# A hybrid encoder trunk on one core: the attention's first unit prepared among the last projections, the weights' tiles at the other end of memory, and the first block's squares added by VectorE

## The chip, the core and the metric

The kernel runs on one core of one Trainium2 chip. The metric is the device time of one execution in microseconds. Beside it stands one profiled execution, whose trace gives every instruction's start and duration on the engines: TensorE (PE), its weight loads (PEld), VectorE (DVE), ScalarE (ACT), GpSimd (POOL) and SyncE (SP), which issues the transfers here.

## The reference

One inference step of one layer over 2048 prompt tokens and 8 x 16 sample tokens, width 1024. One input projection of the normed tokens feeds three groups of heads: forgetting attention (FoX, 6 heads of 64, causal), an RWKV-7 recurrence (6 heads of 64) and cross-attention to 256 memory tokens (4 heads). Each is gated, and one output projection adds the result to the residual.

```python
h = rms_norm(x, norm_g) @ w_in
fox_cols, rwkv_cols, mem_cols = jnp.split(h, [FOX_COLS, FOX_COLS + RWKV_COLS], axis=-1)
# FoX: s = q k / 8 + cq - ck (c: cumulative log forget gates), causal mask, softmax, @ v
# RWKV: S <- S diag(w) + (S @ -kk) (kk a) + v k, y = S r, per-head norm, bonus
# memory: softmax(q mk / 8) @ mv
o = jnp.concatenate([o_f * jax.nn.silu(g_f), o_r * jax.nn.silu(g_r), o_m * jax.nn.silu(g_m)], axis=-1)
y = x + o @ w_out
```

The sample tokens do the same against cached keys and values (512 past rows, 256 memory rows) and a cached recurrent state. Keys, values, log forget gates and the final states are outputs too.

## The kernel before, in words

Precision is kept by splitting a float32 tensor into two parts, hi and lo (`fp32r`): hi is a cast on ScalarE, lo the difference on GpSimd or VectorE, and a product takes three matmuls. The kernel has two stages with a set of pools each.

**Stage 1, projections and recurrence** (pools `p1`, L123 to L942). A loop over four blocks of 512 tokens; the first has the 128 sample tokens as well, so 640. `prep_x` (L225 on) norms a block: squares, their sums over the width, a power, a broadcast back over the partitions, scaling (`stt`, L65) and the split (cast at L279, difference through `tt`, L62). For the first block the sums over partitions are made by PE: ScalarE squares each of the eight 128-row tiles (L251) and a matmul with a column of ones adds each into the tile `pq` (L253), first for 256 tokens, then for 384. `pb` is the broadcast back (L266) and `rb` its copy (L269). The other blocks square rows of tokens (L261). `wd_load` (L176 on) brings 256 columns of `w_in` in two halves of 1 MB, as hi and lo; the first block splits them (raw tile `wraw`, L200 to L202) and writes them to memory in `w_d`, from where the later blocks read them whole (L196). These tiles are in the pool `ws`, four of tag "hl". Projections are `pjd` (columns on the partitions, L209) and `pjt` (tokens on the partitions, `wide`). The columns of the RWKV heads go through `rwkv_in`, `rwkv_mid`, `rwkv_scan` and `rwkv_out` by pairs of heads; the other columns (FoX and memory queries, keys, values, gates) are spread among them. In the last block's last pair stand the memory's normed tokens (`memory_x`), its keys and values ("K", "V") and then the last two gate columns (`g` 0 and 128). `after`, `finish` and `output` close the stage: log forget gates, the last scan, its output.

The scan's PE instructions are named `pa` (first products), `sc` (the state's step), `sy` (its output), `yc` and `pss` (the head norm). The transfers `mk_d`, `mv_d`, `mq_d`, `q_d`, `k_d`, `v_d` and `fg_d` hold projected columns in memory between the stages.

**Stage 2, attention and output projection** (pools `p2`, L943 on). A unit is one pair of heads (`hp`) and 512 queries (`qb`); there are 12 FoX units and 8 of memory attention. A unit's preparation: `fox_keys` loads 512 keys as tokens (`tok`), PE turns them (`pt`, L1004), ScalarE and VectorE split them (L993, L994); `queries` does the same for the queries (L1071, L1072), then one matmul per 128 queries and 512 keys (`pm`) and a maximum over it (L1084 with the mask `mneg`, L1087 without), the maxima negated into `turnm` (L68), turned by PE (`pr`) and put into the queries' tile (L1115), where they are subtracted as part of the logits' matmul. Its main part, `attend`: logits `pS`, the mask, the exponential (L1143), its split (`Ph` by ScalarE, L1146; `Pl` by GpSimd, L62) and the products with the values (`po`). The output projection (`py`) is done for the first weights of w_out (`W`, L1331, tokens `oh`, L1349) early and for the others late; the samples' attention uses the past's keys and values (`sA`, `sB`).

**The order.** Units, memory units, samples and output projections are given fractions in a list `mix` that is sorted; after that `_arrange` puts every instruction of the whole program anew on its engine: a list schedule with a table of costs picks at each step the instruction that can start first, with the program's place as rank, several times over, and keeps the shortest. Tiles of a pool are handed over in the order in which they are asked for, and a pool of stage 2 that lies on the same memory as one of stage 1 waits for the instructions that use it.

## Time and profile before

| | |
| --- | --- |
| three runs | 1807.52, 1809.12 and 1819.66 us, median 1809.12 |
| profiled execution | 1797.65 us |
| its span, first to last instruction | 1795.9 us |
| mean granted clock of PE | 0.972 |
| PE, PEld busy | 94%, 76% of the span |
| DVE, ACT, POOL busy | 54%, 50%, 45% |
| stage 1 ends, stage 2 begins on PE | near 1134 and 1138 us |

A row of the timeline holds the start in the span, the busy time of the instructions taken together, the engine, the line, the operation, output from input, their shape and number (x), and in brackets how long the engine had been idle and what released it. A row of the groups ends with the busy time, the mean of one in nanoseconds, and the idle time before. Names of tiles are the program's. A matmul of `pq`, whose operands are full float32, is two passes in the trace; one of `pjd` is one.

### The profile page before, as it was taken

The numbers are of one execution on the slowest core, as the hardware profiler recorded it, in microseconds if no ns is written. First come the engines' busy times: TensorE is split into PE (matmuls) and PEld (weight loads), VectorE is DVE, ScalarE is ACT, GpSimd is POOL, SyncE is SP. The second block draws the span as 40 slices with busy tenths as digits, with TensorE's granted clock in tenths as the row PEclk, the third lists the DMA queues.
The fourth block names the chain that finished last, engine by engine and source line by source line (L and its number), as shares of the span: only waits on it lengthen the run. The fifth ranks groups of instructions, "written<-read, shape, count | busy, mean of one in ns | idle before, by whom it ended". The sixth has DMA issues, their size and how long they took to land.

```text
span 1795.9 us, 41000 instructions
## 1 busy us (share of the span) xinstructions
PE 1696.7 (94%) x16313; PEld 1362.8 (76%) x16313; DVE 978.1 (54%) x2295; ACT 897.9 (50%) x1783; POOL 811.8 (45%) x824
## 2 busy tenths in 40 slices
PE   7989999999999999999899999799999899999998
PEld 6989989687887788886688887466667666667776
DVE  4654655572454564354574372776745765675214
ACT  5424343523243524233324343588898778886552
POOL 3654543242322242131132151477788566866552
PEclk8999999999999999999999999799999999999999
DMA  6763846653644654644635654534445772444432
GB/s 196 267 202 117 269 144 206 209 178 120 212 156 142 244 184 159 198 155 140 204 109 168 195 160 132 166 121 154 128 149 169 251 251 89 138 142 157 154 111 106
DMA packets 236314, 303.11 MB, mean 169 GB/s; under 512 B 81594, under 2 KB 185976, under 8 KB 220250
## 3 DMA queue, kind: packets, MB, share of 16 engines
q1 hardware_dynamic: 236122, 300.49, 51.5%
q8 instruction: 128, 2.10, 0.5%
q14 instruction: 64, 0.52, 0.1%
HBM read 210.15 MB, written 90.28 MB: 167 GB/s over the span
## 4 chain that ended last, share of the span: by engine, by line
PE 37%; DMA 7%; DVE 7%; ACT 7%; issue 2%; POOL 2%; SPq 1%; DVEq 0%; POOLq 0%; ACTq 0%
PE py L59 8%; PE po L59 6%; PE pjd L59 6%; PE pS L59 5%; PE pjt L59 3%; PE pm L59 2%; ACT P L1143 1%; DMA inv_d<-yt 1%; ACT Ph L1146 1%; POOL Pl L62 1%; DMA sp_d<-spr 1%; DMA xd<-inv_d 1%; DMA rb<-rd 1%; PE pz L59 1%; PE sc L59 1%
## 5 line engine op out<-in xcount | busy, mean ns | idle before, releaser
L59 PE MATMUL pjd<-xk,w 128*128 128x512 f32 (+4 forms) x2280 | 540.2, 378 | 13.0 <-ACT xk L279 4.6
L59 PEld LDWEIGHTS pjd<-xk,w 128*128 128x128 f32 (+1 forms) x2280 | 386.5, 192 | 80.8 <-issue 10.5
L62 POOL TENSOR_TENSOR Pl<-P,Ph 128x512 fp32r<-128x512 f32 (+3 forms) x272 | 318.8, 1183 | 160.6 <-ACT Ph L1146 132.8
L59 PE MATMUL pjt<-w,xk 128*128 128x256 f32 x2040 | 291.4, 290 | 3.9 <-issue 3.9
L59 PEld LDWEIGHTS pjt<-w,xk 128*128 128x128 f32 x2040 | 265.6, 192 | 10.1 <-issue 4.1
L59 PE MATMUL py<-W,oh 128*128 128x512 f32 x816 | 242.6, 399 | 0.9 <-ACT W L1331 0.4
L1143 ACT ACTIVATE P<-pS,NB 128x512 f32<-128x512 f32 x240 | 147.5, 624 | 87.1 <-PE pS L59 34.4
L59 PEld LDWEIGHTS py<-W,oh 128*128 128x128 f32 x816 | 150.9, 189 | 40.1 <-issue 1.0
L59 PE MATMUL pS<-Q,K 128*128 128x512 f32 x480 | 156.6, 387 | 7.1 <-ACT P L1143 4.7
L1146 ACT CAST Ph<-P 128x512 fp32r<-128x512 f32 (+3 forms) x272 | 150.7, 564 | 11.0 <-PE po L59 6.2
L59 PE MATMUL po<-Ph,vt 128*65 128x512 f32 x480 | 153.5, 371 | 2.6 <-ACT ob L1166 1.7
L59 PEld LDWEIGHTS pS<-Q,K 128*128 128x128 f32 x480 | 86.0, 193 | 45.4 <-ACT P L1143 21.6
L1087 DVE TENSOR_REDUCE mx<-pm 128x1 f32<-128x512 f32 x144 | 95.7, 685 | 25.1 <-PE pm L59 23.7
L62 POOL TENSOR_TENSOR nr<-nr,mhalf 128x8 f32<-128x8 f32 (+2 forms) x43 | 62.3, 1448 | 100.3 <-DVE nr L68 87.7
L62 POOL TENSOR_TENSOR w<-wraw,w 128x1024 fp32r<-128x1024 f32 (+1 forms) x34 | 81.6, 2411 | 46.2 <-ACT w L201 33.4
L59 PE MATMUL pm<-K,Q 128*128 128x512 f32 (+2 forms) x240 | 91.2, 399 | 9.2 <-DVE mx L1087 4.0
L59 PE MATMUL po<-Pl,vt 128*65 128x512 f32 x240 | 88.3, 369 | 3.1 <-POOL Pl L62 2.9
L62 DVE TENSOR_TENSOR xo<-py,xo 128x512 f32<-128x512 f32 x68 | 46.2, 685 | 77.9 <-PE py L59 77.6
L59 PEld LDWEIGHTS po<-Ph,vt 128*65 128x65 f32 x480 | 63.4, 136 | 30.9 <-ACT ob L1166 3.3
L62 DVE TENSOR_TENSOR ytmp<-yt 64x14 f32<-64x14 f32 (+9 forms) x210 | 55.0, 262 | 41.8 <-DMA yt<-ld 37.1
L718 ACT COPY qk<-pjt 128x512 f32<-128x512 f32 (+1 forms) x47 | 26.1, 564 | 97.0 <-PE pjt L59 96.7
L59 PEld LDWEIGHTS pm<-K,Q 128*128 128x128 f32 x240 | 46.1, 195 | 31.8 <-DVE mx L1087 11.3
(401 smaller groups left out, 2843.8 us busy)
## 6 DMA issues: line engine op xcount, KB each, us to landing
w<-w_d SPq DMA_DIRECT2D x84, 1024.0 KB
w_d<-w SPq DMA_DIRECT2D x28, 1024.0 KB
y_d<-xo SPq DMA_DIRECT2D x21, 512.0 KB
wraw<-in_w_in SPq DMA_DIRECT2D x36, 256.0 KB
xo<-in_x SPq DMA_DIRECT2D x17, 512.0 KB
xo<-y_d SPq DMA_DIRECT2D x17, 512.0 KB
xt<-in_x SPq DMA_DIRECT2D x24, 256.0 KB
xraw<-in_xT SPq DMA_DIRECT2D x24, 256.0 KB
```

The source lines that it names most:

```text
L59: PE.matmul(out, lhsT, rhs, start=start, stop=stop, skip_group_check=True)
L62: e.tensor_tensor(out=out, in0=a, in1=b, op=op)
L718: S.copy(o_, out)
L1087: V.tensor_reduce(out=to, in_=pm[:, :n], op=MAX, axis=AX.X)
L1143: S.activation(P_[:, c0:], pS[:, c0:], AF.Exp, bias=NB[:, qb, 2 * hp + h, kt:kt + 1] if fox else 0.0)
L1146: S.copy(Ph[:, c0:], P_[:, c0:])
```

## The change

It has four parts.

1. **The first unit** (hp 0, qb 0) is prepared in stage 1. `fox_keys` is cut into `keys` and `values`; the helpers of `queries` take a table `where` that says which tiles they use, `first_` in stage 1 and `late_` in stage 2. `first_unit` gives stage 1's: the keys in one of the four "hl" tiles, the queries in the three `xraw` tiles and `rb`, the tokens in "qk", the mask in "w4", the maxima in "inv", the PSUM tiles in "pj". Keys and queries are emitted ahead of the last pair of gate columns; mask, maxima and negated rows after `after()`, ahead of the last `finish()`. The unit's values stay in stage 2.
2. **The pools** `ws` (weights) and `xr` (new: `xraw` and `rb`) are opened for the whole kernel at the right end of SBUF. Stage 2 uses their tiles: `sA` and `sB` in "hl", the raw output weights and residuals in "w", `ob`, `gt` and `rb2` in `xr`. The tiles of tag "big" fall from seven to five, `turnm` from four to three, the order of stage 2's pools changes.
3. **The first block's squares**: VectorE adds the eight squares of a half into one tile, and PE sums that tile alone, with two matmuls and then three in place of 16 and 24.
4. Smaller tiles: `ssq` halved, three buffers to two for `xss` of k, r and the small columns, two to one for `pb_`.

```diff
-PMB, PSB, PB, HB, LB, LAG, NKB, BIG, POB, PTB = 2, 2, 2, 5, 5, 3, 4, 7, 1, 3
+PMB, PSB, PB, HB, LB, LAG, NKB, BIG, POB, PTB = 2, 2, 2, 5, 5, 3, 4, 5, 1, 3
...
+    ws = pools(ctx, "ws", bufs=WHL, side="right")
+    xr = pools(ctx, "xr", side="right")
...
                     for k in range(KC):
                         sq = sqs[k // 5 if t0 else 0][:, k % 5 if t0 else k, :]
                         S.activation(sq, raws[k][:, c0:c1], AF.Square)
-                        for t in range(t1 - t0):
-                            mm(pq[:, t:t + 1], sq[:, 128 * t:128 * t + 128], one1, start=k + t == 0, stop=k == KC - 1)
+                        if k:
+                            tt(V, sqs[0][:, 0, :], sqs[0][:, 0, :], sq, A_)
+                    for t in range(t1 - t0):
+                        mm(pq[:, t:t + 1], sqs[0][:, 0, 128 * t:128 * t + 128], one1, start=t == 0)
...
+        def first_unit():
+            def k_tiles():
+                m = ws.tile([128, 2048], F32R, tag="hl", name="K0")
+                return [m[:, 512 * h:512 * h + 512] for h in range(2)], [m[:, 512 * h:512 * h + 512] for h in (2, 3)]
+
+            def q_tiles():
+                t_ = [xr.tile([128, 512], F32R, tag="xraw", name="Q0", bufs=3) for _ in range(3)]
+                t_.append(xr.tile([128, 512], F32R, tag="rb", name="Q0"))
+                return t_[:2], t_[2:]
...
+            load, *rest = queries(U0, q0, q_d[0:512, 0:128], 0, 0, True, first_)
+            return [lambda: first_keys[0](0, first_), load, masks, *rest]
...
                             wide(((w, 0), (w, 128)), memx, 2, 0)
+                        if j == len(mine) - 1:
+                            first = first_unit()
+                            for g in first[:2]:
+                                g()
                     f()
         after()
+        for g in first[2:]:
+            g()
         finish()
         output()
...
         def big(name, dtype=F32):
 
+            if name in ("sA", "sB"):
+                return ws.tile([128, 2048], dtype, tag="hl", name=name)
             return lt.tile([128, 2048], dtype, tag="big", name=name, bufs=BIG)
...
         for hp in range(3):
-            U = {}
-            block = fox_keys(U, hp)
+            U, q = ({}, {}) if hp else (U0, q0)
+            keys, values = fox_keys(U, hp) if hp else first_keys
             for qb in range(4):
-                pre, main, end = unit(U, hp, qb, True)
-                units.append(([lambda qb=qb, block=block: block(512 * qb)] + pre, main, end))
+                pre, main, end = unit(U, hp, qb, True, q if not hp and not qb else None)
+                step = [lambda qb=qb, keys=keys, values=values: (keys(512 * qb, late_), values(512 * qb))]
+                if not hp and not qb:
+                    step, pre = [lambda values=values: values(0)], []
+                units.append((step + pre, main, end))
```

The new order is the arranger's, so rows of it are shown, each with its line, operation, output from input and number; line numbers of the changed kernel differ from those of before.

PE at the program's start (`pq` the sums of squares, `pb` the broadcast, `pjd` the first projections). Before:

```order
L59 MATMUL pq<-one_82,xsq 128x1 x16
L59 MATMUL pb<-ident,rsq 128x128 x2
L59 MATMUL pq<-one_82,xsq 128x1 x15
L59 MATMUL pq<-one_82,xsq_247 128x1 x9
L59 MATMUL pjd<-xk,w 70x256 x7
L59 MATMUL pb<-ident,rsq 128x128 x3
L59 MATMUL pjd<-xk,w 70x256 x17
L59 MATMUL pjd<-xk,w 70x384
```

and now:

```order
L58 MATMUL pq<-one_82,xsq 128x1 x2
L58 MATMUL pb<-ident,rsq 128x128 x2
L58 MATMUL pjd<-xk,w 70x256 x4
L58 MATMUL pq<-one_82,xsq 128x1 x3
L58 MATMUL pjd<-xk,w 70x256 x5
L58 MATMUL pb<-ident,rsq 128x128 x3
L58 MATMUL pjd<-xk,w 70x256 x15
L58 MATMUL pjd<-xk,w 70x384
```

The first projections stand around the second half's sums and no longer behind 24 of them.

PE at the end of the last scan (`sc`, `sy`, `yc`, `pss` are the scan's, `pjd` the last pair's projections, 48 in all). Before:

```order
L59 MATMUL sy<-ya,ST 64x64 x2
L59 MATMUL sy<-ya,st 64x64 x14
L59 MATMUL sc<-st,AD 128x64
L59 MATMUL pjd<-xk,w 128x512 x2
L59 MATMUL yc<-yd,centre 128x512
L59 MATMUL pjd<-xk,w 128x512 x4
L59 MATMUL pss<-bones,yd 64x2 x8
L59 MATMUL pjd<-xk,w 128x512 x8
```

and now, with the first unit's transposes (`pt`):

```order
L148 MATMUL pt<-ident,tok 128x128
L58 MATMUL sc<-st,AD 128x64 x2
L58 MATMUL sy<-ya,ST 64x64 x2
L58 MATMUL sy<-ya,st 64x64 x14
L58 MATMUL sc<-st,AD 128x64
L58 MATMUL yc<-yd,centre 128x512
L58 MATMUL pss<-bones,yd 64x2 x8
L58 MATMUL pjd<-xk,w 128x512 x16
```

No projection stands between the scan's last steps now; all 48 follow `pss`. On SP, where the pair's two weight loads are issued (`w<-w_d`), before:

```order
L196 DMA w<-w_d 128x2048
L767 DMA fg_d<-gth 128x512
L196 DMA w<-w_d 128x2048
L726 DMA mk_d<-qk 128x2x256
L726 DMA out_mk_p<-qk 128x2x256
L767 DMA fg_d<-gth 128x512
L726 DMA mv_d<-qk 128x2x256
```

and now:

```order
L878 DMA mk_d<-qk 128x2x256
L878 DMA out_mk_p<-qk 128x2x256
L919 DMA fg_d<-gth 128x512
L145 DMA tok<-k_d 128x4x128
L878 DMA mv_d<-qk 128x2x256
L346 DMA w<-w_d 128x2048 x2
L145 DMA tok<-q_d 128x4x128
```

The loads stand behind the memory's keys and values and the first unit's key tokens.

ACT at the attention's beginning (`P` an exponential, `Ph` its cast, K and Q the casts of keys and queries, `W` of the output weights). Now:

```order
L1208 ACTIVATE P<-pS,NB 128x128
L1211 CAST Ph<-P 128x128
L137 CAST K_13952<-pt 64x512
L219 CAST Q_13989<-pt 64x512
L138 CAST K_13954<-pt 64x512
L220 CAST Q_13991<-pt 64x512
L1398 CAST W<-wr 128x1024
L137 CAST K_13953<-pt 64x512
```

where before, ahead of the first exponential:

```order
L993 CAST K_13963<-pt 64x512
L1013 CAST vt<-vtok 128x8x64
L994 CAST K_13965<-pt 64x512
L1071 CAST Q_14000<-pt 64x512
L1072 CAST Q_14002<-pt 64x512
L993 CAST K_13964<-pt 64x512
L1331 CAST W<-wr 128x1024
L1071 CAST Q_14001<-pt 64x512
```

The second unit's casts have moved from ahead of the first unit's exponentials to behind its eighth.

More of the change, by code (lines that the diff above doesn't have):

```diff
@@ new lines, in turned_in, with values_in @@
+    def turned_in(src, n, where):
+        t_ = where["tok"]()[:, :n // 128]
+        SY.dma_start(t_, src.rearrange("(t p) c -> p t c", p=128))
+        pt = where["pt"]("pt")
+        for t in range(n // 128):
+            PE.transpose(pt[:, 128 * t:128 * t + 128], t_[:, t, :], ident)
+        return pt
+    def values_in(vt, vsrc, nt):
+        t_ = c2.tile([128, 4, 2, 64], F32, tag="tok", name="vtok", bufs=3)[:, :nt]
+        SY.dma_start(t_, vsrc.rearrange("(t p) (h d) -> p t h d", p=128, d=64))
+        G.memset(vt[:, 0:130 * nt].bitcast(F32), 1.0)
+        v1 = vt[:, 0:130 * nt].rearrange("p (t h d) -> p t h d", h=2, d=65)
+        v2 = vt[:, 130 * nt:258 * nt].rearrange("p (t h d) -> p t h d", h=2, d=64)
+        S.copy(v1[:, :, :, 0:64], t_)
+        tt(V, v2, t_, v1[:, :, :, 0:64].bitcast(F32), SUB)
+        return v1, v2
@@ new lines, in fox_keys, with keys, values @@
+    def fox_keys(U, hp):
+        cs = slice(128 * hp, 128 * hp + 128)
+        U["K1"], U["K2"], U["vt"] = [], [], []
+        def keys(g0, where):
+            gs = slice(g0, g0 + 512)
+            pt = turned_in(k_d[gs, cs], 512, where)
+            k1, k2 = where["K"]()
+            for h in range(2):
+                split_keys(k1[h], k2[h], pt[64 * h:64 * h + 64], 512)
+                SY.dma_start(k1[h][64:67, :].bitcast(F32), nc_d[2 * hp + h:2 * hp + h + 13:6, gs])
+            U["K1"].append(k1)
+            U["K2"].append(k2)
+        def values(g0):
+            vt = kv.tile([128, 1032], F32R, tag="vt", name="vt", bufs=NKB)
+            U["vt"].append(values_in(vt, v_d[g0:g0 + 512, cs], 4))
+        return keys, values
@@ L168 @@
         xs_ = pools(p1, "xs")
-        ws = pools(p1, "ws", bufs=WHL)
         pj = pools(p1, "pj", bufs=3, space=bass.MemoryType.PSUM)
@@ L944 @@
         lt = pools(p2, "lt", bufs=2)
-        fill = lt.tile([128, FILL], BF16, tag="fill", name="fill", bufs=1) if FILL else None
+        kp = pools(p2, "kp")
+        wk = pools(p2, "wk", bufs=2)
+        lp = pools(p2, "lp", bufs=2)
         c2 = pools(p2, "c2")
@@ L1160, in values @@
                     if not R:
-                        R["ob"] = lt.tile([128, 512], F32, tag="ob", name="ob")
+                        R["ob"] = xr.tile([128, 512], F32, tag="xraw", name="ob", bufs=3)
                         R["sd"] = dt("sd", [2, 512], bufs=2)
@@ L1184, in ending @@
             def ending():
-                rb, gt = (lt.tile([128, 512], F32, tag=t_, name=t_, bufs=1) for t_ in ("rb2", "gt"))
+                rb, gt = (xr.tile([128, 512], F32, tag=t_, name=n_, bufs=b_) for t_, n_, b_ in (("rb", "rb2", 1), ("xraw", "gt", 3)))
                 SY.dma_start(gt, gsrc)
```

305 lines of the change are left out of this document (152 added, 153 removed).

## The prediction

> **What bounds the kernel now.** I read the shares of the page first, then the slices, then the table of windows over the two places that the change touches, then the timeline there.
>
> ```profile
> span 1795.9 us, 41000 instructions
> PE 1696.7 (94%) x16313; PEld 1362.8 (76%) x16313; DVE 978.1 (54%) x2295; ACT 897.9 (50%) x1783; POOL 811.8 (45%) x824
> PE   7989999999999999999899999799999899999998
> PEclk8999999999999999999999999799999999999999
> 20.00:30.00 10.00, 9.56 (x52) 9.30 (x52) 4.28 (x17) 2.05 (x5) 2.59 (x3) 1.00 0.69 207
> 30.00:40.00 10.00, 4.49 (x14) 2.84 (x14) 8.20 (x19) 8.15 (x22) 2.67 (x3) 0.71 0.54 180
> 40.00:50.00 10.00, 8.88 (x38) 7.53 (x39) 5.65 (x6) 5.53 (x12) 9.89 (x6) 0.61 0.80 256
> 50.00:60.00 10.00, 8.37 (x56) 8.14 (x56) 8.13 (x17) 5.41 (x13) 4.29 (x7) 1.00 0.99 341
> 1100.00:1125.00 25.00, 25.00 (x381) 21.31 (x380) 7.34 (x17) 7.93 (x17) 4.83 (x4) 1.00 0.46 149
> 1125.00:1150.00 25.00, 16.88 (x82) 12.16 (x81) 14.81 (x34) 13.35 (x27) 11.79 (x20) 0.73 0.68 210
> 1150.00:1175.00 25.00, 20.61 (x72) 13.01 (x73) 24.72 (x58) 17.70 (x37) 13.14 (x16) 0.72 0.34 110
> 1175.00:1200.00 25.00, 24.37 (x121) 16.95 (x120) 16.30 (x37) 22.65 (x41) 17.53 (x17) 1.00 0.38 116
> ```
>
> PE is busy 94% of the span, so only places where it idles or runs below its full clock can give time. The slices show few: the first, and the one with a 7 in both rows near two thirds. A window's row holds its length, the busy time of PE, PEld, DVE, ACT and POOL, the granted clock, and the share and rate of the DMA. PE's busy time times its clock over 1125 to 1175 is 16.88 x 0.73 + 20.61 x 0.72 = 27.2 us of 50, so some 23 us are lost where the projections hand over to the attention. From 30 to 50 it is 4.49 x 0.71 + 8.88 x 0.61 = 8.6 of 20. From 50 on, and again from 1175 on, PE is nearly full at full clock. The change works on both holes.
>
> **Part 1: the first block's squares.** Now every square is summed over the 128 partitions by PE; 40 such matmuls are 80 passes in the trace.
>
> ```profile
> 4.57 6.98 PE L59 MATMUL pq<-one,xsq 128*128 128x1 f32 x32 [4.57 <-ACT xsq L251]
> 10.10 0.52 ACT L251 ACTIVATE xsq<-xraw 128x384 f32<-128x384 f32 x1 [0.52 <-DMA xraw<-in_xT]
> 14.25 1.28 DVE L65 SCALAR_TENSOR_TENSOR xraw<-xraw,vec,rb 128x256 f32<-128x256 f32 x3 [2.51 <-ACT rb L269]
> 14.27 10.40 PE L59 MATMUL pq<-one,xsq 128*128 128x1 f32 x48 [0.46 <-ACT rb L269]
> 24.54 1.75 PE L59 MATMUL pjd<-xk,w 128*70 128x256 f32 x7
> 33.74 0.40 PE L59 MATMUL pjd<-xk,w 128*70 128x384 f32 x1 [4.18 <-ACT xk L279]
> 39.62 5.01 POOL L62 TENSOR_TENSOR w<-wraw,w 128x1024 fp32r<-128x1024 f32 x2 [3.21 <-ACT w L201]
> 51.11 6.18 PE L59 MATMUL pjd<-xk,w 128*128 128x384 f32 x39 [0.90 <-DVE fl L62]
> ```
>
> The two pq rows are 17.38 us for 80 passes, 0.217 each; 10 passes remain, 2.2 us, so PE gives up 15.2 us. VectorE takes 14 adds; its nearest row is 1.28 / 3 = 0.43 us for 128x256, and by width 0.64 at most for 128x384, so 7 x 0.43 + 7 x 0.64 = 7.5 us, on an engine that is busy for 4.28 us of 10 from 20 to 30. They run behind the squares one by one, so that of each half only the last add, 0.4 and 0.6, lies on the path.
>
> What it brings is not 15.2, since other things must be there. In the first half the sum is ready when PE has drained, at 4.57 + 6.98 = 11.55. ScalarE has by then done squares of the second half (10.10). In the changed order the last token tile of the first half is loaded behind two loads of the second and squared behind one square of the second, so I put its square at about 9.4 and its add at 9.9: a gain of 1.7 us. The second half: the pq passes end at 24.67, and the first 128x384 projection begins at 33.74; without the passes it can begin near 26, so 7.7 us sooner. Next in line is the split of the next weights on Pool (39.62 to 44.63), which itself waits for ScalarE's cast of them and those for the tokens' tiles; if it moves with the rest, to about 37.5, it gains 7.1. From 51.11 PE is full, so whatever is gained there is kept. The term is **-7.1 us**. Bounds: 0 if a transfer sets the pace (the DMA share is 0.99 at 341 GB/s from 50 to 60), and the whole 10.40 us of the second pq row on the other side.
>
> **Part 2: the hand-over.** The first unit's keys, queries and eight maxima are made among the last pair's projections, in their tiles. The cover it takes away is that of the last scan. I count from the last scan's first "pa" matmul ("pa" at 1110.78, with as much PE work left on both sides).
>
> ```profile
> 1082.80 0.79 PE L59 MATMUL pjd<-xk,w 128*128 128x512 f32 x1 [3.08 <-DMA w<-w_d]
> 1076.74 0.54 SPq L196 DMA_DIRECT2D w<-w_d  x1
> 1110.78 1.15 PE L59 MATMUL pa<-bt,za 64*64 64x64 f32 x32
> 1118.86 0.36 SPq L726 DMA_DIRECT2D mv_d<-qk  x1
> 1125.00 0.63 PE L59 MATMUL pss<-bones,yd 128*64 128x2 f32 x16
> 1129.95 4.13 PE L59 MATMUL pjd<-xk,w 128*128 128x512 f32 x17
> 1138.08 1.11 PE L1004 MATMUL pt<-ident,tok 128*128 128x128 f32 x4 [4.00 <-DVE gth L65]
> 1146.60 0.30 DVE L1084 CUSTOM_DVE_ANT_0 pm<-pm,mneg 128x128 f32<-128x128 f32 x1
> 1152.59 0.13 DVE L1084 DVE_READ_ACCUMULATOR2_ANT mx<- 128x1 f32 x1
> 1157.97 0.69 ACT L1143 ACTIVATE P<-pS,NB 128x512 f32<-128x512 f32 x1 [2.10 <-DVE pS L62]
> 1172.80 2.53 PE L59 MATMUL py<-W,oh 128*128 128x512 f32 x7
> 1178.02 0.48 PE L59 MATMUL pS<-Qm,Km 128*128 128x512 f32 x1
> ```
>
> A pass of the last pair costs 4.13 / 17 = 0.243 us. Before, 16 of its 48 passes fill the scan's waits and the last ends at 1134.08, 23.3 after pa. In the changed order none of the 48 stands ahead of pss, because the pair's two weight loads are issued behind mv_d (1118.86); a load of that kind was used 1082.80 - 1076.74 = 6.1 us after its issue, so the first half is there 14.2 after pa. pss ends at 1125.63, 14.9 after pa, and then come 48 x 0.243 = 11.7 and four transposes of 0.28: the last pass ends 27.7 after pa, **4.4 later** than before.
>
> What follows it is shorter. Before, 23.9 us pass from the last pass to the first exponential (1157.97): tokens back from memory, transposes, casts, maxima. Now the casts are done by then; left are the first maximum's matmul (1.1), eight maxima (VectorE's own work between 1146.60 and 1152.72, without the pauses for PE and for a scan of the sample's forget values, is 3.5), and from the last maximum to the first exponential as before, 1157.97 - 1152.72 = 5.3: 9.9 together, so 14.0 saved. The first exponential comes 27.7 + 9.9 = 37.6 after pa and not 47.2: **9.6 sooner**.
>
> That isn't the gain, for the second unit's preparation moves the other way. Before, its keys' and queries' eight casts and two of w_out's stand on ScalarE ahead of the first exponential. Now they stand behind the first unit's eighth. By the rows
>
> ```profile
> L1143 ACT ACTIVATE P<-pS,NB 128x512 f32<-128x512 f32 x240 | 147.5, 624 | 87.1 <-PE pS L59 34.4
> L1146 ACT CAST Ph<-P 128x512 fp32r<-128x512 f32 (+3 forms) x272 | 150.7, 564 | 11.0 <-PE po L59 6.2
> 1139.23 0.58 ACT L993 CAST K<-pt 64x512 fp32r<-64x512 f32 x1 [0.49 <-PE pt L1004]
> 1148.55 1.04 ACT L1331 CAST W<-wr 128x1024 fp32r<-128x1024 f32 x1
> ```
>
> eight exponentials with their casts are at most 8 x (0.624 + 0.564) = 9.5 (narrower ones less: I take 9), and the ten casts 8 x 0.58 + 2 x 1.04 = 6.7. So the second unit's casts, its maxima and its exponentials wait for 9 of the 9.6 and come 0.6 sooner than before. The early output projections (py, 1172.80) need only the last two of these casts and could begin some 5 sooner; the first memory logits (1178.02) stand behind the second unit's casts on ScalarE and follow them. What counts is when PE is full for good, which the memory logits mark: I take **0 us**. Bounds: -9.6, if PE finds work beside the second unit's casts, and +9: the 4.4 lost, and half of the 9 besides.
>
> **Part 3: the attention.** Pools at memory's other end let the past's keys and values (sA, sB) start loading in the last projections, where before
>
> ```profile
> 1400.00:1425.00 25.00, 21.23 (x106) 13.90 (x105) 22.93 (x61) 17.80 (x37) 13.23 (x18) 0.86 0.91 286
> PE pS L59 <- DMA sB<-in_cmkT: 0.7, 2, 0.5
> ```
>
> the window with their use loses 25 - 21.23 = 3.8 us of PE at DMA share 0.91, of which the wait itself shows 0.7. Against it stand five big tiles where there were seven, so that a memory unit's queries can't be prepared two ahead. PE's order in the rest is the same by units. I take **-1**: from -3.8, the window's whole loss, to +3.8, as much again where a memory unit's queries come late. Edits without a time of their own: masks read as two planes, smaller rows for squares, one buffer less for shifted columns; they are small beside the scans that hide them, and would cost a VectorE instruction's 0.3 each if not.
>
> **Sum.** -7.1 + 0 - 1 = -8.1. On the profiled execution's 1797.65 (span 1795.9 and 1.75 around it) that is 1789.6. The median of the runs is 1809.12, 11.5 above the profiled one, with 12 us between the lowest and the highest; so I subtract from the median: **1801.0 us**.
>
> [...] The row after the 4.00 us wait above is
>
> ```profile
> 1140.00:1145.00 5.00, 2.73 (x10) 1.75 (x8) 3.24 (x5) 4.06 (x9) 2.91 (x7) 0.50 1.03 294
> 1155.00:1160.00 5.00, 4.93 (x16) 3.42 (x15) 4.92 (x12) 2.46 (x5) 0.86 (x1) 0.50 0.38 111
> ```
>
> half clock from 1140 to 1160, 20 us. [...]
>
> **Rivals.** A, the hand-over pays in full (PE has the first unit's values, py and transposes to do while ScalarE casts): -7.1 - 9.6 - 1 = -17.7, 1791.4. For it: py's rows could begin 5 us sooner. Against: VectorE was 24.72 of 25 busy from 1150 to 1175, so it is no free engine there.
> B, the start gives only its first 1.7: the weights' loads and ScalarE's squares of the second block set the pace there; -1.7 + 0 - 0 = 1807.4. For it: ScalarE 8.15 of 10 and the DMA at 0.99. Against: the 4.18 us wait was for xk, not for a transfer.
> C, slower: the last pair's weights. Their loads queue behind mv_d with the first unit's own tokens and w_out's; if the first lands 6 us later than I say, PE has no work after the scan, and the 48 passes run at half clock, 11.7 us more: 6 + 11.7 - 7.1 - 1 = +9.6, 1818.7. It decides once PE idles over 4 us ahead of the pair. Against: the DMA share there is 0.46 from 1100 to 1125.
> D, the planner puts the maxima behind everything anyway, and only part 1 works: -7, which is the forecast's time.
>
> **How the numbers follow.** Forecast (with D) 0.50, A 0.25, B 0.14, C 0.11. A spread of 5 us around each is the runs' own. The range 1784 to 1818 takes in A, B and the bounds of part 1, and leaves out the far side of A and most of C. A measurement here tells about 1% from no change, 18 us. Over 1% faster is half of A, and the forecast with both of its terms at their good bounds: 0.29. Over 1% slower is the tail of C: 0.12. Within 1%: 0.59.
>
> **What would show it.** In the profile after: pq passes 10, the first 128x384 projection near 26 and PE full from about 44; the last pair's passes in one run behind pss, its clock 1.00; the first exponential about 10 us nearer to the last scan, and the first memory logits no nearer. It is wrong if the last pair waits for its weights (C), if the memory logits come 8 us sooner too (A), or if the wait for xk near 30 stands with another name (B).

## The result, and the profile after

| | before | after |
| --- | --- | --- |
| median of four runs each, on one chip | 1808.85 us (1807.52 to 1819.66) | 1827.32 us (1824.57 to 1830.33) |
| profiled execution, its span | 1797.65, 1795.9 us | 1824.57, 1822.8 us |

The ratio is 1.0088, interval 1.0062 to 1.0114: 16 us slower by the ratio, and 18.5 by the medians. I had said 8.1 faster, with 1784 to 1818 as the range. The loss is under 1%, but its interval lies wholly above 1, the sign is not the one I gave, and the time lies outside the range.

The page of the kernel after: the busy shares, and PE's two rows of slices.

```profile
PE 1691.6 (93%) x16243; PEld 1347.3 (74%) x16243; DVE 984.0 (54%) x2309; ACT 895.1 (49%) x1784; POOL 805.1 (44%) x824
PE   5789997989999999999989999879999999999998
PEclk9899998999999899999999999889999999999999
```

PE has 5 us less to do (1691.6 against 1696.7) and the span is 26.9 longer, so what grew is the time in which PE idles; the mean granted clock is 0.972 in both. Three places show in the slices: the first two (5 and 7, where there were 7 and 9), the seventh (7 at clock 8, at 273 to 319 us) and the hand-over (8 and 7).

The start, in two of the windows that the prediction used for before: length, busy time of PE, PEld, DVE, ACT and POOL, granted clock, DMA share and rate.

```profile
40.00:50.00 10.00, 6.90 (x32) 5.90 (x32) 4.19 (x7) 0.81 (x3) 3.81 (x2) 0.72 0.58 190
50.00:60.00 10.00, 3.28 (x12) 3.19 (x13) 6.86 (x18) 6.69 (x15) 5.49 (x6) 0.62 1.05 382
```

PE was to be full from about 44; from 50 to 60 it is busy for 3.28 of 10 at clock 0.62, where before it had 8.37 at 1.00. The rows of the timeline of after, PE and ACT, in the order of time:

```profile
30.29 0.59 PE L58 MATMUL pjd<-xk,w 128*70 128x384 f32 x1 [1.85 <-ACT xk L431]
49.91 1.04 ACT L351 CAST w<-wraw 128x1024 fp32r<-128x1024 f32 x1 [3.23 <-DMA wraw<-in_w_in]
50.98 0.47 ACT L468 COPY fsb<-pjd 6x384 f32<-6x384 f32 x1
51.51 0.34 PE L471 MATMUL pf<-ident,fsb 6*128 6x6 f32 x3 [4.17 <-ACT fsb L468]
57.07 3.25 PE L58 MATMUL pjd<-xk,w 128*128 128x384 f32 x9 [5.22 <-DVE xsk L64]
```

The first wide projection does begin 3.4 sooner (30.29 for 33.74). Then PE waits 4.17 us for `fsb`, a small copy on ScalarE that stands in its queue behind a cast of weights; that cast had itself waited 3.23 for its transfer. Behind it PE waits 5.22 more, and is full from 57.07 and not from 51.11.

The next place lies between 200 and 400 us, on which the prediction said nothing. The two windows of before, and those of after:

```profile
200.00:300.00 100.00, 97.79 (x1199) 91.77 (x1199) 60.50 (x143) 40.12 (x85) 46.61 (x43) 1.00 0.59 194
300.00:400.00 100.00, 94.97 (x1139) 77.98 (x1137) 56.54 (x145) 39.62 (x89) 28.73 (x32) 0.97 0.59 188
```

```profile
200.00:300.00 100.00, 90.37 (x1112) 82.38 (x1108) 46.32 (x122) 37.30 (x80) 40.92 (x39) 0.93 0.56 178
300.00:400.00 100.00, 87.27 (x1009) 72.20 (x1010) 51.05 (x131) 36.01 (x84) 18.39 (x24) 0.93 0.48 159
```

Busy time by clock is 189.9 before and 165.2 after. What is late there is seen in the view of one tile, `xssk` (a pair's shifted sample columns; each row has its least, median and longest time, and the start of the first and the last of the three pairs). `bk` is the last to read it. Before, then after:

```profile
L307 POOL COPY xssk<-shp x3: 200/202/672, 56.5 to 213.5; 128x8 f32<-128x8 f32 x3
L65 DVE SCALAR_TENSOR_TENSOR bk<-xssk,vh,e x3: 350/350/1090, 322.1 to 842.8; 128x128 f32<-128x128 f32 x3
```

```profile
L459 POOL COPY xssk<-shp x3: 199/201/207, 64.8 to 332.5; 128x8 f32<-128x8 f32 x3
L64 DVE SCALAR_TENSOR_TENSOR bk<-xssk,vh,e x3: 350/352/353, 332.1 to 869.5; 128x128 f32<-128x128 f32 x3
  DVE bk L64: 5.5, 1
```

All three pairs write such a tile in the first block, and the first pair's is read when its sample unit runs, behind the third pair. With three buffers the third write stands at 213.5, with two at 332.5, right behind the first pair's `bk` at 332.1: the last row says that Pool sat idle 5.5 us for that `bk`. So the third pair's samples, written 119 us later, hold back the end of the first block. The next block's tokens, the eight casts of `xk` of 512, tell by how much. Before, then after:

```profile
L279 ACT CAST xk<-xraw x8: 609/619/621, 311.9 to 337.8; 128x512 fp32r<-128x512 f32 x8
```

```profile
L431 ACT CAST xk<-xraw x8: 602/618/622, 360.4 to 379.6; 128x512 fp32r<-128x512 f32 x8
```

The first is 48 us later. This is the smallest edit of the change, the one that the prediction put among those "without a time of their own".

To set whole kernels beside each other I cut each trace where PE has done the same amount of matmul work (sums of squares left out, each shape at the duration that it has back to back). The reference is a second run of the kernel before, `b_same` below, since its profiled execution of 1797.65 lies 11 under the median; its cuts are at 63.8, 219.8, 427.3, 1124.5 and 1206.9 us of 1802.0. With other durations for the shapes an entry moves by up to some 3 us. Microseconds lost (+) or gained (-) against it:

| kernel | to 64 | to 220 | first block's end, to 427 | to 1124 | hand-over, to 1207 | attention | span |
| --- | --- | --- | --- | --- | --- | --- | --- |
| before, first profile | +2.1 | +0.3 | +0.2 | -10.2 | +0.2 | +1.2 | -6.1 |
| after | +9.8 | -0.3 | +14.9 | -4.6 | +8.1 | -7.1 | +20.8 |
| after_t14 | -0.5 | -0.9 | +12.3 | +6.0 | +12.0 | +0.1 | +29.0 |
| after_t4 | +1.9 | -2.7 | +15.0 | -3.7 | +11.3 | +2.3 | +24.0 |
| a_xss3 | +5.7 | -7.5 | -3.1 | -20.8 | +11.2 | +5.9 | -8.6 |
| a_xss3_t5 | +2.2 | +1.3 | -1.4 | -16.4 | +9.2 | -3.7 | -8.8 |
| a_xss3_unit1 | +2.7 | +3.1 | -0.8 | -16.6 | +9.7 | +4.7 | +2.8 |
| a_xss3_late | +1.9 | +3.6 | -2.3 | -14.5 | +2.5 | -2.7 | -11.7 |
| a_xss3_pq | +1.9 | +2.9 | -1.6 | -8.3 | +12.3 | +6.0 | +13.1 |
| a_xss3_kept | +8.9 | -0.3 | +13.2 | -2.1 | +12.2 | -5.1 | +26.8 |
| a_samp01 | +2.9 | +4.5 | -5.0 | +4.5 | +8.0 | +4.5 | +19.3 |
| a_samp01_t16 | +1.2 | +1.8 | -3.4 | -13.5 | +7.3 | +0.7 | -5.9 |
| a_pq | +2.1 | +6.9 | +18.4 | +1.9 | +8.2 | +3.5 | +41.1 |
| b_xss2 | +3.6 | 0.0 | +9.3 | -6.3 | -2.9 | +2.2 | +5.9 |
| b_adds_xss2 | +1.3 | +1.8 | +7.9 | -1.3 | -1.1 | +12.8 | +21.5 |
| b_adds | +6.8 | -2.3 | -6.7 | -9.6 | -1.5 | -2.7 | -16.0 |
| b_adds_t4 | +1.0 | +2.8 | -2.2 | -5.6 | -0.1 | +1.3 | -2.8 |
| b_adds_kept | -0.7 | +3.4 | -2.2 | -2.1 | -0.1 | +3.6 | +1.9 |
| b_try2 | +0.9 | +9.8 | -3.8 | -13.2 | +3.9 | +5.3 | +3.1 |

The first row is the same program twice: 10 us in one column is within what a run does.

### The profile page after: what moved, and what is told of

Its sections match the earlier page's. It is cut to its first block, busy times and chain, and to the rows that moved or that the text cites. A ratio compares the mean times of both kernels' runs of the same rounds, so it can differ in the third digit from the quotient of the medians.

```text
span 1822.8 us, 40919 instructions
## 1 busy us (share of the span) xinstructions
PE 1691.6 (93%) x16243; PEld 1347.3 (74%) x16243; DVE 984.0 (54%) x2309; ACT 895.1 (49%) x1784; POOL 805.1 (44%) x824
## 4 chain that ended last, share of the span: by engine, by line
PE 56%; DMA 12%; DVE 10%; ACT 8%; issue 4%; SPq 2%; POOL 2%; DVEq 0%; ACTq 0%; POOLq 0%
PE pjd L58 15%; PE py L58 8%; PE pjt L58 7%; PE po L58 7%; PE pS L58 4%; PE pm L58 2%; ACT P L1208 2%; DMA w<-w_d 2%; PE sc L58 1%; ACT Ph L1211 1%; DMA AR<-sp_d 1%; PE gr L58 1%; PE pz L58 1%; DMA yd<-sp_d 1%; DMA inv_d<-yt 1%
## 5 line engine op out<-in xcount | busy, mean ns | idle before, releaser
L58 PE MATMUL pjd<-xk,w 128*128 128x512 f32 (+5 forms) x2280 | 551.0, 382 | 40.0 <-DMA w<-w_d 7.1
L58 PEld LDWEIGHTS pjd<-xk,w 128*128 128x128 f32 (+1 forms) x2280 | 390.4, 193 | 112.1 <-issue 12.8
L58 PE MATMUL pS<-Q,K 128*128 128x512 f32 (+1 forms) x480 | 156.4, 389 | 8.6 <-ACT P L1208 5.6
L235 DVE TENSOR_REDUCE mx<-pm 128x1 f32<-128x512 f32 x144 | 95.5, 684 | 27.7 <-PE pm L58 26.7
L61 POOL TENSOR_TENSOR xk<-xraw,xk 128x512 fp32r<-128x512 f32 (+2 forms) x20 | 23.8, 1188 | 82.4 <-ACT xk L431 82.4
```

Of the source, the lines that this page charges most:

```text
L58: PE.matmul(out, lhsT, rhs, start=start, stop=stop, skip_group_check=True)
L61: e.tensor_tensor(out=out, in0=a, in1=b, op=op)
L235: V.tensor_reduce(out=to, in_=pm[:, :n], op=MAX, axis=AX.X)
```

## The experiments

**Theories.** One: two buffers for `xss` of k, r and the small columns make the first block end late, and that is the loss. Two: the first unit's early preparation costs it in the hand-over, because the second unit comes late. Three: neither, but the order that `_arrange` happens to keep, since any edit changes it everywhere. The expectations call one A, three B and two H; their C is that the adds and what they do to the start are the cost. Names with b_ are the kernel before with an edit, those with a_ the changed kernel. Medians are those of the runs, each ratio is against before on the same chip, and a comparison of two kernels rests on their medians.

### Buffers and adds, each alone and undone

`b_xss2` takes the two buffers into before, `b_adds` the adds, `b_adds_xss2` both. `a_xss3` gives the changed kernel its third buffer back (for room, the first unit's negated rows lie in a scan tile, and stage 2 has three of its own), `a_pq` takes the adds out, `a_xss3_pq` does both.

```diff
-name="xss" + key, bufs=3)
+name="xss" + key, bufs=3 if key in "gv" else 2)
...
+            rows0 = rw.tile([128, 512], F32R, tag="e5", name="rows0")
```

> The kernel before with one edit: the tiles of the sample tokens' shifted columns (xss of k, r and the small columns) have two buffers and not three. Theory A (the two buffers are what cost stage 1 its time: the third pair's sample columns must wait until the first pair's sample unit has read its own, and the order of the whole first block bends around that): slower than before by 15 to 20 us, about 1826, with the loss between 200 and 400 us of the span. Theory B (any edit makes the arranger pick another order and the changed kernel's loss is chance): anywhere from 10 us faster to 20 slower, with the loss in no fixed place. Theory C (the adds on VectorE and what they do to the start are the cost): no change within 4 us.

> The kernel before with the first block's squares added by VectorE and summed by 5 matmuls, nothing else changed. Theory A: the adds are not the loss; from no change to 7 us faster (the first projections at 30 us sooner, a part of it kept). Theory B: anywhere within 20 us. Theory C: 8 us slower or more, with ScalarE's copy of the forget columns behind a cast that waits for its weights, near 50 us.

> The changed kernel with three buffers again for xss of k, r and the small columns; to make room, the first unit's negated rows and the rounded identity lie in a scan tile (e5) and stage 2 has its own again. Theory A: 15 to 20 us faster than the changed kernel, 1807 to 1812, with stage 1 as long as before and the hand-over still some 10 us longer. Theory B: anywhere within 20 us of the changed kernel. Theory C: as the changed kernel, 1827, within 4 us.

> The changed kernel with the 40 sums on PE as before and no adds on VectorE. Theory A: within 5 us of the changed kernel, 1822 to 1832, since the loss of the first block stays. Theory B: anywhere within 20 us. Theory C: 8 to 15 us faster than the changed kernel, 1812 to 1819, with PE full from 51 us as before.

> The changed kernel with three buffers for xss of k, r and the small columns (1795.9 us so far) and the first block's sums on PE as before, no adds. If the adds are worth some 17 us in every surrounding (they were 16.5 on the kernel before and 17.6 on the changed one): 1811 to 1815. If that was chance of the order, with the adds' own effect read at the start alone (3 to 8 us lost there): 1786 to 1794.

> The kernel before with the adds (1790.8 us so far) and two buffers for xss of k, r and the small columns. Theory A (the third pair's sample columns wait for the first pair's sample unit, whatever stands around): 14 to 31 us slower than with three, 1805 to 1822, the loss between 200 and 300 us of the span. If the two buffers cost 5 us, as the median on the kernel before had it: 1796.

| other parts of the change | sums by | three buffers | two buffers |
| --- | --- | --- | --- |
| none | PE | 1807.4 (before) | 1813.3, 1.0023 [0.9996, 1.0051] |
| none | VectorE | 1790.8, 0.9894 [0.9856, 0.9933] | 1818.0, 1.0062 [1.0034, 1.009] |
| early unit, pools | PE | 1817.3, 1.0055 [1.0025, 1.0085] | 1844.9, 1.0201 [1.016, 1.0241] |
| early unit, pools | VectorE | 1795.9, 0.9932 [0.9904, 0.9960] | 1827.3, 1.0088 [1.0062, 1.0114] (after) |

The third buffer, with the moves that make room for it, turns the changed kernel from slower to faster than before. Two buffers cost 5.9, 27.2, 27.6 and 31.4 us in the four pairs. The other differences in the table have no fixed size either: the adds bring 16.6, 21.4 and 17.6 us and cost 4.7 in the pair of before with two buffers, and the early unit with the pools costs 5.1, 9.3, 9.9 and 31.6. The pools had no run of their own.

Most of what was expected missed. `b_xss2` lost 5.9 us and not 15 to 20, with an interval that includes 1; `b_adds` gained 16.5 where A allowed 7 at most; `a_xss3` came 11 below A's range and `a_pq` 13 above it; `a_xss3_pq` lay above both of its ranges. `b_adds_xss2` was within A's. C is out, since the changed kernel is 17.6 slower without the adds. So no theory gave the size of the medians; what the traces do show is where the time is lost. The tile view and the windows of `a_xss3`:

```profile
L456 POOL COPY xssk<-shp x3: 200/200/201, 60.8 to 217.2; 128x8 f32<-128x8 f32 x3
L64 DVE SCALAR_TENSOR_TENSOR bk<-xssk,vh,e x3: 344/352/353, 320.3 to 829.4; 128x128 f32<-128x128 f32 x3
200.00:300.00 100.00, 98.07 (x1189) 92.33 (x1188) 59.94 (x145) 38.05 (x83) 44.70 (x42) 0.98 0.61 199
300.00:400.00 100.00, 93.55 (x1154) 77.07 (x1153) 60.82 (x151) 40.57 (x92) 29.12 (x33) 1.00 0.57 185
```

The third write is back at 217.2, and busy time by clock at 189.7. In `b_xss2`:

```profile
L307 POOL COPY xssk<-shp x3: 195/200/204, 58.6 to 326.2; 128x8 f32<-128x8 f32 x3
L65 DVE SCALAR_TENSOR_TENSOR bk<-xssk,vh,e x3: 346/350/351, 325.8 to 857.8; 128x128 f32<-128x128 f32 x3
200.00:300.00 100.00, 90.77 (x1114) 82.28 (x1113) 52.61 (x137) 38.43 (x82) 43.36 (x43) 0.95 0.53 173
300.00:400.00 100.00, 93.45 (x1107) 75.45 (x1107) 53.69 (x130) 38.86 (x89) 19.21 (x29) 0.98 0.54 181
```

The same mark without any other part of the change: third write at 326.2 behind `bk` at 325.8, and 177.8 of work where before had 189.9. In the table of cuts the six kernels with two buffers and the sample units where they were all lose there, 7.9 to 18.4 us (after 14.9); the eleven with three buffers, but for the one whose order was kept from two, are between -6.7 and +0.2. Theory one holds for the place. The medians differ by more than the place does, which is the next question.

### How much is the order alone?

`_arrange` tries several times and keeps its shortest. `b_try2`, `after_t14`, `after_t4`, `a_xss3_t5` and `b_adds_t4` keep another one of its tries, nothing else (each with a number of its own in the line below). `b_adds_kept` and `a_xss3_kept` let the edit in but keep every engine's order as before or as after had it (a table of ranks; in `a_xss3_kept` the instructions of the first unit's rows alone are placed anew); `b_same` is before by such a table.

```diff
-    _, start = min(found, key=lambda x: x[0])
+    _, start = found[4]
```

> The kernel before, same program, but the arranger keeps its second best order and not its best; by its own sums that order is 5.9 us longer (1637.9 and 1632.0). If the chip follows those sums: 4 to 8 us slower, 1811 to 1815. Theory B (which order is kept is worth as much as the edits): off by more than 8 us in either direction.

> The kernel before, with its own order given as a table of ranks: the same work in the same order. Within 3 us of before; a second profile of it, since the first one's execution was 10 us shorter than the median of the runs.

> The kernel before with the adds, every engine's order kept as before (ranks from a table); the adds stand behind their squares on VectorE, and 35 sums are gone from PE. If the adds themselves are worth the 16.6 us of the version whose order was made anew: 1791. If that came with the other order, and the start is set by the weights' loads and casts, as its trace has it: within 4 us of before, 1804 to 1811.

> The changed kernel with three buffers for xss, but every engine's order kept as the changed kernel has it (a table of ranks takes the place of the arranger's own; only the instructions of the first unit's rows are placed anew). If the two buffers cost by the waits for a tile at run time: as fast as with the order made anew, 1796 to 1805. If they cost by the order that they force (sample unit ahead, projections behind), which is kept here: within 5 us of the changed kernel, 1822 to 1832.

> The changed kernel, unchanged, with another of the arranger's 18 orders kept (its own sums: 1653.6 against 1652.4 for the one kept so far). If the two buffers cost in any order (the third pair's sample columns must follow the first pair's sample unit): 1820 to 1845, with the loss of 10 us or more between 150 and 300 of the matmul work there again. If the changed kernel's time was chance of its one order: under 1812.

> As the run before, with a third order, from another group of the arranger's tries (1654.6 by its sums): 1820 to 1845 if the two buffers cost in any order, under 1812 if it was chance.

> The changed kernel with three buffers for xss and another of the arranger's orders (1635.0 by its sums against 1633.3). If the third buffer gives the time back in any order: 1790 to 1812, no loss in the first block. If 1795.9 was chance: anywhere up to 1830.

> The kernel before with the adds, another of the arranger's orders (1631.7 by its sums against 1627.9). If the adds bring 16 us by what they free: 1787 to 1797. If it was chance of the one order: 1800 to 1815.

| kernel | first order | other order | order kept |
| --- | --- | --- | --- |
| before | 1807.4 | 1805.2, 0.9989 [0.9973, 1.0004] | 1806.1, 0.9987 [0.9965, 1.0009] |
| before, adds | 1790.8 | 1800.3, 0.9959 [0.9925, 0.9993] | 1809.2, 0.9991 [0.9973, 1.0009] |
| changed | 1827.3 | 1826.1, 1827.9: 1.0102 [1.0062, 1.0142], 1.0103 [1.0068, 1.0138] | |
| changed, three buffers | 1795.9 | 1800.5, 0.9941 [0.9914, 0.9968] | 1826.6, 1.0092 [1.006, 1.0124] |

Three orders with two buffers lie within 2 us of each other, 26 to 32 above two orders with three buffers, so the loss is no accident of one order. But the third buffer gives nothing where the order stays that of two (1826.6). The tile view of `a_xss3_kept`:

```profile
L456 POOL COPY xssk<-shp x3: 202/203/207, 63.9 to 323.6; 128x8 f32<-128x8 f32 x3
L64 DVE SCALAR_TENSOR_TENSOR bk<-xssk,vh,e x3: 351/351/353, 328.7 to 867.8; 128x128 f32<-128x128 f32 x3
```

The third write no longer waits for `bk`, it stands ahead of it, and is late all the same. So the price is not waiting at run time, it is the order that the missing buffer forces on the arranger. The adds give nothing in the order of before (1809.2), and 9 to 17 in an order of their own; the 9 of `b_adds_t4` (1800.3 beside 1809.5 for before on its chip) is at the edge of what was written down as chance of one order. By the cuts, the mean of the three two-buffer rows less that of the two three-buffer rows is 33.3: 16.3 at the first block's end, 17.8 in the three blocks behind it, and the others together less than 1. No buffer is short in that second stretch, and one program differs by 10 there from run to run. Why the orders that follow are worse there stays open.

### The sample unit put elsewhere, two buffers kept

The first pair's sample unit runs behind the second pair and not behind the third, so its tile is free before the third writes. `a_samp01_t16` is the same with another of the tries.

```diff
-SAMP = ((0, 2), (1, 2), (2, 2))
+SAMP = ((0, 1), (1, 2), (2, 2))
```

> The changed kernel, two buffers as it has them, with one edit: the first pair's sample unit stands behind the second pair's columns in the program and no longer behind the third's (first entry of SAMP), so that its tiles are read before the third pair's columns need them. Theory A (the two buffers cost by making the third pair's sample columns wait for the first pair's sample unit): most of the loss returns without a third buffer, 10 to 25 us faster than the changed kernel, 1802 to 1817, the loss between 200 and 350 us gone. Rival (the two buffers cost in other ways, or by the order at large): within 6 us of 1827.

> The changed kernel with two buffers and the first pair's sample unit behind the second pair's columns, another of the arranger's orders (1637.4 by its sums against 1637.3). With the first order the loss of the first block was gone but the time was as before it, by losses in the last block and the hand-over. If those were chance of the order: 1800 to 1818. If something in this edit costs there: 1822 or more again, with the loss in the same places.

1826.4, 1.0090 [1.0052, 1.0127], and 1807.1, 0.9983 [0.9958, 1.0008]. The tile view of `a_samp01_t16`:

```profile
L459 POOL COPY xssk<-shp x3: 193/200/202, 55.6 to 242.3; 128x8 f32<-128x8 f32 x3
L64 DVE SCALAR_TENSOR_TENSOR bk<-xssk,vh,e x3: 339/352/2508, 239.8 to 840.3; 128x128 f32<-128x128 f32 x3
```

The tile is read at 239.8 and written again at 242.3, 90 us sooner than in after, and both lose nothing at the first block's end (-5.0, -3.4). So the lifetime is the cause there, not the memory's place. As a whole the first of them took the time that the rival gave (within 6 of 1827), and the second is 19 below it. Most of the difference lies in the three blocks behind, +4.5 against -13.5: either order alone would have misled, and how much of the whole loss the lifetime accounts for is not shown by these two.

### The first unit late, and the second early

`a_xss3_late` has three buffers, adds and pools, and prepares the first unit in stage 2 as before. `a_xss3_unit1` is `a_xss3` with the second unit's preparation ranked with the first's values, so that its casts stand behind the fourth exponential and not the eighth.

```diff
-        spread(units[0][0], -1, 0, 0)
+        spread(units[0][0] + units[1][0], -1, 0, 0)
...
-            if j < 11:
+            if 0 < j < 11:
```

> The changed kernel with three buffers for xss and the first unit prepared in stage 2 as before; adds and pools as changed. Theory H (the early preparation uncovers the last scan and puts the second unit's casts behind the first unit's exponentials, 10 us in the three traces that have it): 8 to 11 us faster than 1795.9, 1785 to 1788, the difference between the last scan and the first memory logits. Rival: the 10 us are given back in the attention, where those traces gained up to 10: within 4 us of 1795.9.

> The changed kernel with three buffers for xss, and the second unit's preparation ranked with the first unit's, ahead of its main part and no longer spread over it; in the new order its casts stand behind the first unit's fourth exponential and no longer behind the eighth. If the hand-over is longer because the second unit's casts wait: its share of 8 to 12 us (matmul work 800 to 850) falls to 3 to 7 us, and the whole to 1789 to 1796. Rival (the hand-over is longer because the last pair's projections no longer fill the scan): still 8 to 12 us there.

1795.4, 0.9928 [0.9903, 0.9952], against 1795.9 with the early unit; and 1803.0, 0.9959 [0.993, 0.9987]. The first is the rival's time and not H's 1785 to 1788; the second lies above the 1789 to 1796 that was written down for late casts. As a whole the early unit is worth nothing that I can measure, but its own price is not in that: by the cuts `a_xss3` is 14.4 us ahead of `a_xss3_late` up to 1124, where little of the early unit stands, and 17.3 behind it from there on. In the hand-over all eleven kernels with it lose 7.3 to 12.3; those without lie between -2.9 and +3.9. The four windows of 20 us from the last scan's first `pa`, in `b_same`, in after and in `a_xss3_unit1`:

```profile
1118.30:1138.30 20.00, 20.00 (x257) 16.65 (x257) 4.18 (x13) 5.72 (x11) 1.88 (x2) 1.00 0.14 50
1138.30:1158.30 20.00, 11.77 (x41) 8.00 (x39) 14.32 (x33) 11.58 (x23) 10.15 (x19) 0.65 0.82 254
1158.30:1178.30 20.00, 15.71 (x56) 9.39 (x56) 19.78 (x48) 12.96 (x26) 11.52 (x14) 0.76 0.33 105
1178.30:1198.30 20.00, 19.38 (x90) 13.34 (x90) 12.87 (x29) 18.29 (x36) 10.65 (x13) 0.92 0.42 134
```

```profile
1138.70:1158.70 20.00, 17.70 (x241) 14.32 (x240) 5.00 (x12) 6.60 (x12) 1.22 (x3) 1.00 0.65 227
1158.70:1178.70 20.00, 15.61 (x55) 10.13 (x55) 12.28 (x40) 8.88 (x18) 8.53 (x11) 0.75 0.73 229
1178.70:1198.70 20.00, 14.74 (x51) 8.87 (x50) 11.55 (x22) 15.27 (x29) 10.52 (x18) 0.67 0.39 121
1198.70:1218.70 20.00, 16.21 (x61) 10.66 (x62) 17.95 (x42) 13.01 (x27) 5.56 (x10) 0.73 0.43 130
```

```profile
1115.40:1135.40 20.00, 18.43 (x182) 14.24 (x180) 6.50 (x16) 7.90 (x15) 3.63 (x4) 1.00 0.62 219
1135.40:1155.40 20.00, 10.97 (x37) 6.38 (x35) 12.75 (x38) 5.40 (x11) 6.88 (x10) 0.60 0.75 226
1155.40:1175.40 20.00, 16.24 (x54) 11.05 (x54) 15.41 (x34) 16.65 (x35) 11.62 (x20) 0.63 0.44 140
1175.40:1195.40 20.00, 18.86 (x78) 13.19 (x78) 14.61 (x30) 17.64 (x33) 11.88 (x13) 0.83 0.31 98
```

Busy time by clock over the 80 us is 57.4, 51.1 and 50.9. In `a_xss3_unit1` the second unit is in time (ninth exponential 66.1 us behind `pa`, 65.9 in `b_same`, 75.4 in after), and the loss is still there. So a late second unit is no sufficient cause, and theory two falls in that form.

The rival written down for this run, that the last pair's projections no longer fill the scan, said 8 to 12 us and 9.7 came. The windows show it in part: in the first one, where the scan runs, PE has 17.7 and 18.4 us of work done against 20.0, which is 2.3 and 1.6 of the 6.3 and 6.5 lost.

What the kernels with the early unit share besides is the clock. Over the 100 us from the last scan's first `pa` its mean is 0.78 to 0.85 in the eleven with it and 0.85 to 0.91 in the nine without (0.83 in after, 0.86 in `b_same`). The slow stretches of after, then of `a_xss3_late`, which has no early unit:

```profile
1168.70:1185.60 16.90, 12.46 (x42) 7.89 (x42) 9.19 (x26) 8.42 (x17) 5.54 (x10) 0.50 0.68 211
1185.70:1192.40 6.70, 3.92 (x20) 1.98 (x18) 1.89 (x5) 5.76 (x12) 5.34 (x8) 1.00 0.47 150
1192.50:1209.40 16.90, 12.68 (x29) 7.26 (x30) 16.40 (x33) 12.80 (x25) 5.70 (x12) 0.50 0.55 166
```

```profile
1132.80:1146.40 13.60, 4.18 (x13) 3.19 (x14) 6.13 (x8) 5.86 (x10) 3.83 (x9) 0.50 1.04 345
1146.40:1153.20 6.80, 4.07 (x18) 2.32 (x16) 5.86 (x16) 5.86 (x12) 2.63 (x6) 1.00 0.51 160
1153.20:1163.40 10.20, 8.51 (x26) 5.91 (x27) 9.46 (x25) 7.34 (x15) 1.73 (x4) 0.50 0.36 103
```

In after the clock comes back for 6.7 us, in which PE has 3.92 to do, and then stands at 0.50 for as long again. It is tempting to read the loss so: one unit alone fills PE, lets it run dry and costs a second stretch at half clock. But `a_xss3_late` has a second stretch too and loses 2.5 us here, and `a_xss3`, with the early unit, has one of 34.0 us (1126.2 to 1160.2) and one of 6.8 and loses 11.2. So more time at half clock goes with the early unit, and the second stretch does not mark it. Why the clock stays low for longer is open; a kernel in which the first unit's gap is filled was not among the runs.

## Why the prediction was wrong

**The failed step: "one buffer less for shifted columns"**, which I put at nothing, "small beside the scans that hide them". I priced the instructions and not the lifetime: three writes in the first block, and a first reader that stands behind all of them. It measured +14.9 us in place (12.3 and 15.0 in the changed kernel's other orders), and with what follows 5.9 to 31.4 in the medians of the four pairs, 31.4 in the changed kernel's own. It could have been seen without a run: in the tile view of before, `bk` first reads at 322.1, and the third write at 213.5 stands ahead of it; that needs three buffers.

**The start, -7.1**, was +9.8 in after, and -0.5 and +1.9 in its other orders. In after alone this term is further off than that of the buffers (16.9 us against 14.9), but the buffers' loss comes in all three orders and this one does not. The matmuls did go and the first wide projection came 3.4 sooner. What rival B says of the weights' loads is seen in after: the cast at 49.91 waited for its transfer, and PE for the copy behind that cast. It is not the only limit. In `b_adds_kept`, with the order of before, the start gives 0.7 us and the kernel nothing. Its rows of PE in the first 33 us:

```profile
22.58 1.41 PE L59 MATMUL pq<-one,xsq 128*128 128x1 f32 x6 [8.27 <-DVE xsq L62]
32.62 0.39 PE L59 MATMUL pjd<-xk,w 128*70 128x384 f32 x1 [1.78 <-ACT xk L281]
```

PE waits 8.27 us for the adds where it had summed for 10.40, and the first wide projection comes 1.1 sooner, not 7.7. The squares are done there at 16.4, but the adds stand among VectorE's other work, the last from 21.36 to 22.43; so "only the last add, 0.4 and 0.6, lies on the path" did not hold in this order. What `b_adds` gains as a whole is not the start (+6.8 there) but the stretches behind, and in the order of before it is gone; I put it down to the order.

**The hand-over, 0.** The steps themselves held: first pass of the last pair predicted 14.9 behind `pa`, last pass 27.7, first exponential 37.6; measured in after 14.2, 26.8 and 37.6. What failed is "come 0.6 sooner" of the second unit. Its ninth exponential came 75.4 behind `pa` against 65.9, 9.5 later. The rows of after:

```profile
1138.66 1.15 PE L58 MATMUL pa<-bt,za 64*64 64x64 f32 x32
1176.26 0.69 ACT L1208 ACTIVATE P<-pS,NB 128x512 f32<-128x512 f32 x1 [1.70 <-DVE pS L61]
1189.61 0.58 ACT L137 CAST K<-pt 64x512 fp32r<-64x512 f32 x1 [0.27 <-DMA o_d<-bv]
1214.07 1.27 ACT L1208 ACTIVATE P<-pS,NB 128x512 f32<-128x512 f32 x2
```

The second unit's first cast comes 13.4 us behind the first unit's first exponential, 1176.26 to 1189.61, and not 9. ScalarE is busy for 8.79 of them, so the work was sized rightly; the rest is waiting, with PE at a mean clock of 0.65, which I put at nothing. From that cast another 24.5 us pass to the ninth exponential; I set the wait against the first exponential, though before the casts had ended well ahead of it. The bound of +9 that I gave holds +8.1. Yet `a_xss3_unit1` loses 9.7 with the second unit in time, so this step's correction is not the whole cause, and the rest of it stays open.

**The attention, -1**, was -7.1 in after, +0.1 and +2.3 in its other orders: nothing that can be told from run and order. Rival C has the right sign and the wrong place: the last pair's weights were there at 14.2 behind `pa`, as the forecast had it. Rivals A and D are out.

**The base.** The profiled execution of 1797.65 lay 11 us under the median. I subtracted from the median, and that was right: `b_same`, the same instructions in the same order, has a span of 1802.0 and a median of 1806.1.

## What to carry to other kernels

Price a buffer taken away by its tile's lifetime, from its write to its last reader in the profile before, and count how many writes stand ahead of that reader; an order that a scheduler makes will bend around it with hardly a wait to be seen (5.5 us here). Where a scheduler rewrites the whole order, run an edit in two or three of its orders and once in the kept order before it gets credit: here one edit's two orders differed by up to 19 us. The fastest versions are before with the adds alone (1790.8) and the changed kernel with its third buffer (1795.9, and 1795.4 with the first unit late), all below the two kernels compared, with a part of that being the order's luck.

## What the runs showed of the hardware

One program's executions spread by 10 us and more without any change: 29 of before in one session on one chip lay between 1799.83 and 1820.02, and those of all sessions between 1792.15 and 1821.58.

The granted clock can stay at half while the profile shows PE busy without a gap. In before:

```profile
351.70:355.10 3.40, 3.40 (x30) 2.64 (x29) 2.29 (x6) 2.01 (x5) 1.38 (x2) 0.50 0.42 120
355.10:358.50 3.40, 3.40 (x21) 2.24 (x21) 0.33 (x2) 2.78 (x9) 1.67 (x2) 0.50 0.15 29
358.50:361.90 3.40, 3.40 (x16) 2.77 (x16) 0.00 (x0) 0.00 (x0) 0.05 (x1) 1.00 0.44 128
```

PE is busy for all of 6.8 us and has half clock throughout. In after it is busy for all of 3.30 us from 950.2 at 0.50, and the next 3.30, from 953.6, are at 1.00; in `a_xss3_unit1` it is busy for 4.00 of 4 us from 1156 at 0.50, and the next window of 4 is at 0.93. So the busy time at half clock ahead of the full rate was not of one length, 3.3 us in after and 6.8 in before, and what sets it is not shown. Beside the prediction's row of 4.93 busy us of 5 at 0.50, the same trace has a plainer case in these 6.8 us.
